# Dilated attention: mixing weights broadcast through a DRAM scratch instead of by selector products

## The chip, the cores and the metric

The kernel runs on one core of one Trainium2 chip. What counts is the time of one execution on the device, in microseconds; the median of several runs is given. The core has TensorE (matrix products), VectorE, ScalarE, GpSimd, and SyncE, whose queue issues nearly all DMA transfers.

## The reference

Two layers of a hybrid attention block over 512 tokens of width 1024. A layer normalises x, multiplies it by one wide matrix, runs three attentions, gates and merges them, and adds the result to x. The change is in the third attention, the dilated mixture: three groups of four heads (64 wide) attend with different windows and strides, and their outputs are mixed per token and head by a softmax over the three groups' log-sums:

```python
C_GROUPS = ((128, 1), (512, 4), (2048, 16))
def dilated_mixture(q, k, v):
    outs, lses = [], []
    for g, (window, dil) in enumerate(C_GROUPS):
        o, l = dilated_group(q[:, :, sl], k[:, :, sl], v[:, :, sl], window // dil, dil)
        outs.append(o); lses.append(l)
    w = jax.nn.softmax(jnp.stack(lses, axis=0), axis=0)      # 3 groups x tokens x 4 heads
    return jnp.sum(w[..., None] * jnp.stack(outs, axis=0), axis=0).astype(q.dtype)
...
    yc = dilated_mixture(...).reshape(bsz, seq, C_WIDTH) * jax.nn.silu(c_g)
    merged = (gates[:, :, 0] * (ya @ w_br_a) + gates[:, :, 1] * (yb @ w_br_b) + gates[:, :, 2] * (yc @ w_br_c))
    return x + merged @ w_out
```

## The kernel before

All large products are made of three: both operands are split into a high part (rounded to the product's format) and a low part, and hi*hi, lo*hi and hi*lo are added up in PSUM (lines 430 to 432 for blocks of 128 features by 512 tokens). Activations stand transposed, features on the partitions, tokens along the row. Weights come from DRAM as `ws` tiles (4 buffers) by SyncE's queue, ScalarE (sometimes VectorE) casts them to `whi`, and GpSimd (sometimes VectorE) subtracts to get `wlo`; `whi` and `wlo` have 7 buffers each, so weights run ahead of the products by a few tiles. Products go to PSUM buffers: three for blocks (`pp`), two for scores (`sc`), two for transposes (`tp`), one for attention outputs (`pv`).

The order of the instructions is not written by hand. The kernel lists its operations with an engine, an assumed duration, what they read and write and a priority; a planner (class `Plan`) plays them through, always taking the operation that can start first, and the engines' instruction streams are emitted in the order it found. Each engine, and SyncE's queue, works its stream strictly in order. Operations of the attentions have their own priorities, projections and merges ("fills") take the room between them, and weight loads come first on SyncE (priority about -1e5).

Within a layer the units follow this list: `CV K I V Q D0 D1 A1 CW T C01 C00 gC gA gB A0 AB0 AB1 AB2 AA0 AA1 VR C1 C2 A2 AA2 B1 B0 MX B2`. MX (`c_mix`) is the mixing. For each group g and pair of heads pr there is an output `U[g][pr]`, 128 partitions (two heads of 64) by 512 tokens. The weights are worked out with tokens on the partitions (tile C, 12 columns per 128 tokens), and four transposes give them as 12 rows by 512 tokens in PSUM (`tpm`, line 1080). To multiply U by them, each row has to stand on all 64 partitions of its head. Before the change the 12 rows are split into `rw` (high part in rows 0 to 11, low part in rows 32 to 43, the rest zeroed), and a product with a constant selector of zeros and ones puts two rows onto 64 partitions each:

```python
bc = buf("sc", [P, T], F32, "bc")
nc.tensor.matmul(bc.t, sel.t[0:64, 2 * g + pr, :], rw.t[0:64], start=True, stop=True)   # L1094
add("dve", n_dve(T), lambda u=u, bc=bc: vt(u.t, u.t, bc.t, ALU.mult), r=[u, bc], w=[u], pri=pri)
```

That is six products a layer, each followed by VectorE's multiply from PSUM (line 1064). GpSimd then adds the three U of a pair, multiplies by the gate, and the result is split into `yh` and `yl`, the operands of branch B2. Around the mixing TensorE works on the gates and products of branch B0 (gate blocks of 24 products, branch products of 9); VectorE's line 873 merges them.

The selector `sel` is set up once near the start: three tiles zeroed, six small loads into them, three casts.

Of the kernel before, what the change touches and what calls it, by code (L numbers as in the profile page):

```python
# [16 lines left out]
P = 128  # L17
T = 512
# [196 lines left out]
def n_act(n, fn=False):  # L215
    return 0.84 * n + (290 if fn else 165)


def n_pool(n):
    return 2.15 * n + 190  # L220
# [3 lines left out]
def hybrid_kernel(ctx: ExitStack, tc, x, norm_g, w_in, w_br_a, w_br_b, w_br_c, w_out, final_norm_g,  # L224
# [13 lines left out]
    def buf(tag, shape, dt=F32, name="t"):  # L238
        counter[0] += 1
        return Buf(tag, shape, dt, f"{name}_{counter[0]}")  # L240

    def fixed(shape, dt, name):
        b = Buf(None, shape, dt, name)
        b.t = sb.tile(shape, dt, name=name, tag=name)
        return b
# [8 lines left out]
    tri = fixed([P, T], F32, "tri")  # L254
    band = fixed([P, 256], F32, "band")
    res = fixed([P, P], F32, "res")
    sel = fixed([P, 6, P], FR, "sel")
    scol = fixed([P, 1], F32, "scol")
    invd = fixed([P, 4], F32, "invd")
    big = fixed([P, 1], F32, "big")  # L260
    x1 = tc.dram_tile([T, D], F32, name="x1")
    vdram = [tc.dram_tile([T, T], F32, name=f"vd{l}") for l in range(DEPTH)]
    vdtok = [[token(f"vd{l}{t}") for t in range(4)] for l in range(DEPTH)]
    x1tok = [[token(f"x1_{t}{b}") for b in range(2)] for t in range(4)]
# [40 lines left out]
            add("act", 60, lambda: nc.scalar.dma_start(ident.t, k_ident), w=[ident], pri=-7e5, lag=3200.0)  # L305
    for b, k in ((cos, k_cos), (sin, k_sin), (tri, k_tri), (band, k_band), (res, k_res)):
        dma(lambda b=b: b.t, lambda k=k: k, b, 300, pri=50)
    for g in range(3):

        s32 = buf("u", [P, 2, P], F32, "s32")  # L310
        add("pool", 300, lambda s32=s32: nc.gpsimd.memset(s32.t, 0.0), w=[s32], pri=50)
        for p0 in (4 * g, 32 + 4 * g):
            dma(lambda s32=s32, p0=p0: s32.t[p0:p0 + 4], lambda: k_sel[32:36], s32, 300, pri=50)
        add("act", n_act(256), lambda g=g, s32=s32: nc.scalar.copy(sel.t[:, 2 * g:2 * g + 2, :], s32.t), r=[s32], w=[sel], pri=50)
    add("pool", 100, lambda: nc.gpsimd.memset(scol.t[0:64], -0.125), w=[scol])
    add("pool", 100, lambda: nc.gpsimd.memset(scol.t[64:128], 1.0), w=[scol])
    add("pool", 100, lambda: nc.gpsimd.memset(invd.t, 1.0 / D), w=[invd])
# [430 lines left out]
    def layer(l):  # L748
# [306 lines left out]
        def c_mix(gC):  # L1055
# [24 lines left out]
                    nc.tensor.transpose(tp.t[0:12, i, :], C.t[:, 12 * i:12 * i + 12], ident.t)  # L1080
            add("pe", n_mm(4, P), ft, r=[C, ident], w=[tp], pri=pri, name="mixT")

            rw = buf("u", [P, T], FR, "rw")
            add("pool", n_pool(T) / 2, lambda: nc.gpsimd.memset(rw.t[0:64].bitcast(F32), 0.0), w=[rw], pri=pri, after=plan.ops[-1:])
            split(lambda: tp.t[0:12].rearrange("p b n -> p (b n)"), tp, lambda: rw.t[0:12], rw, lambda: rw.t[32:44], rw, T, pri, True)
            ys = []
            for pr in range(2):
                acc = None
                for g in range(3):
                    pri = apri()  # L1090
                    bc = buf("sc", [P, T], F32, "bc")

                    def fb(pr=pr, g=g, bc=bc):
                        nc.tensor.matmul(bc.t, sel.t[0:64, 2 * g + pr, :], rw.t[0:64], start=True, stop=True)  # L1094
                    add("pe", n_mm(1, T), fb, r=[rw, sel], w=[bc], pri=pri, name="bc")
                    u = U[g][pr]
                    add("dve", n_dve(T), lambda u=u, bc=bc: vt(u.t, u.t, bc.t, ALU.mult), r=[u, bc], w=[u], pri=pri)
                    if acc is None:
                        acc = u
                    else:  # L1100
                        tt(T, lambda acc=acc: acc.t, lambda acc=acc: acc.t, lambda u=u: u.t, ALU.add, [u, acc], [acc], pri, "cadd")
                tt(T, lambda acc=acc: acc.t, lambda acc=acc: acc.t, lambda pr=pr: gC[pr].t, ALU.mult, [acc, gC[pr]], [acc], pri, "cgate")
                yh, yl = buf("u", [P, T], FR, "yh"), buf("u", [P, T], FR, "yl")
                split(lambda acc=acc: acc.t, acc, lambda yh=yh: yh.t, yh, lambda yl=yl: yl.t, yl, T, pri)
                ys.append((yh, yl))
# [127 lines left out]
```

## Time and profile before

| | |
|---|---|
| median of 3 runs | 1074.54 us (1073.83 to 1074.83) |
| profiled execution, its own time | 1073.64 us |
| its span, first to last instruction | 1071.9 us |
| TensorE busy / weight loads | 1062.5 us / 885.9 us |
| VectorE, ScalarE, GpSimd busy | 510.9, 592.0, 637.5 us |
| granted TensorE clock | 0.998 of full |
| moved by DMA | 119.00 MB |

The span is that of the one execution that was profiled; its own time is the device time of the same execution. Busy times are sums of the instructions' durations; a product's recorded duration (about 390 ns for 512 columns) overlaps with the next one's, so the distance between two starts is what a product takes.

### The profile page before, as it was taken

To read this page: it belongs to the slowest core of one execution; us is meant where nothing else is said; L and a number is where in the kernel's file an instruction comes from. 1 tells how busy PE (TensorE), PEld (TensorE's weight loads), DVE (VectorE), ACT (ScalarE), POOL (GpSimd) and SP (SyncE) were. 2 spreads that over 40 slices of the span, in tenths; PEclk is the share of its full clock that TensorE was granted. 3 is DMA by queue.
4 is the path that set the end of the run, shared out by engine and by line. 5 is a ranking of instruction groups with operands and counts; after the bars stand their busy time and mean duration, and the time that the engine had idled before them with its cause. 6 is when DMAs were issued, how large, how long until landed. Compare 5 with 4: busy or idle time off the path is not lost.

```text
span 1071.9 us, 16877 instructions
## 1 busy us (share of the span) xinstructions
PE 1062.5 (99%) x5390; PEld 885.9 (83%) x5390; DVE 510.9 (48%) x1434; ACT 592.0 (55%) x1493; POOL 637.5 (59%) x636
## 2 busy tenths in 40 slices
PE   9999999999999999999999999999999999999997
PEld 5898888888887878888888889888888878788885
DVE  5138987566642441113432589856655425311143
ACT  6444356787776653334553444568877767333441
POOL 4765754557753349776666177545666425686853
PEclk9999999999999999999999999999999999999999
DMA  7653543433431323453754155334444223336322
GB/s 227 186 125 79 148 109 83 140 83 94 120 94 51 81 60 99 110 175 98 217 160 130 30 136 145 85 95 112 112 101 119 65 52 81 87 89 194 109 81 78
DMA packets 123690, 119.00 MB, mean 111 GB/s; under 512 B 19385, under 2 KB 102225, under 8 KB 123602
## 3 DMA queue, kind: packets, MB, share of 16 engines
q1 hardware_dynamic: 123312, 117.61, 40.3%
q8 instruction: 42, 0.69, 0.3%
q14 instruction: 46, 0.38, 0.1%
q10 hardware_dynamic: 290, 0.33, 0.1%
HBM read 96.07 MB, written 6.36 MB: 96 GB/s over the span
## 4 chain that ended last, share of the span: by engine, by line
PE 98%; ACT 1%; issue 1%; DVE 0%; POOL 0%; POOLq 0%
PE pp L430 22%; PE pp L432 21%; PE pp L431 21%; PE sc L542 4%; PE pp L451 3%; PE pp L450 3%; PE pp L449 3%; PE po L1150 3%; PE po L1149 3%; PE po L1151 3%; PE tp L614 2%; PE pv L637 2%; PE pv L649 1%; PE sc L999 1%; PE pv L1037 1%; PE tpn L717 1%
## 5 line engine op out<-in xcount | busy, mean ns | idle before, releaser
L337 POOL TENSOR_TENSOR wlo<-ws,whi 128x256 fp32r<-128x256 f32 (+2 forms) x439 | 439.4, 1016 | 314.7 <-ACT whi L331 260.9
L430 PE MATMUL pp<-h_hi,whi 128*128 128x512 f32 (+1 forms) x896 | 357.1, 399 | 0.4 <-DVE gate L526 0.3
L432 PE MATMUL pp<-h_hi,wlo 128*128 128x512 f32 (+1 forms) x896 | 348.4, 389 | 0.0
L431 PE MATMUL pp<-h_lo,whi 128*128 128x512 f32 (+1 forms) x896 | 348.2, 389 | 0.0
L331 ACT CAST whi<-ws 128x256 fp32r<-128x256 f32 (+2 forms) x434 | 214.7, 508 | 236.1 <-PE pp L431 123.8
L432 PEld LDWEIGHTS pp<-h_hi,wlo 128*128 128x128 f32 x896 | 168.2, 188 | 35.1
L430 PEld LDWEIGHTS pp<-h_hi,whi 128*128 128x128 f32 x896 | 168.5, 188 | 34.3 <-issue 3.5
L431 PEld LDWEIGHTS pp<-h_lo,whi 128*128 128x128 f32 x896 | 168.6, 188 | 28.7
L873 DVE SCALAR_TENSOR_TENSOR th<-th,pp 128x512 f32<-128x512 f32 x32 | 22.0, 687 | 132.0 <-PE pp L432 126.8
L390 DVE TENSOR_TENSOR ptl<-tp,pth 128x256 fp32r<-128x256 f32 (+3 forms) x128 | 58.1, 462 | 44.0 <-ACT pth L331 43.3
L449 PE MATMUL pp<-whi,h_hi 128*128 128x512 f32 (+2 forms) x192 | 67.5, 352 | 0.0
L451 PE MATMUL pp<-whi,h_lo 128*128 128x512 f32 (+2 forms) x192 | 66.8, 348 | 0.0
L450 PE MATMUL pp<-wlo,h_hi 128*128 128x512 f32 (+2 forms) x192 | 66.7, 347 | 0.0
L331 ACT CAST pth<-tp 128x256 fp32r<-128x256 f32 (+3 forms) x128 | 50.7, 406 | 26.1 <-PE tp L614 15.0
L858 ACT ACTIVATE th<-pp 128x512 f32<-128x512 f32 x48 | 28.6, 595 | 54.6 <-PE pp L432 54.6
L552 ACT ACTIVATE p<-p,st 128x128 f32<-128x128 f32 (+3 forms) x96 | 53.5, 558 | 1.8 <-DVE st L550 1.5
L609 ACT ACTIVATE p<-p,st 128x128 f32<-128x128 f32 (+3 forms) x96 | 50.9, 558 | 1.8 <-DVE st L608 1.4
L820 DVE MATCH_REPLACE8 work<-m,work 128x512 f32<-128x512 f32 (+2 forms) x96 | 51.8, 542 | 0.1
L819 DVE MAX8 m<-work 128x8 f32<-128x512 f32 (+2 forms) x96 | 50.8, 550 | 0.7 <-POOL work L812 0.4
L430 PE MATMUL pp<-yh,whi 128*128 128x512 f32 x128 | 50.7, 396 | 0.0
L1149 PE MATMUL po<-whi,mhh 128*128 128x512 f32 x128 | 50.2, 392 | 0.0
L432 PE MATMUL pp<-yh,wlo 128*128 128x512 f32 x128 | 50.0, 391 | 0.0
(189 smaller groups left out, 1732.3 us busy)
## 6 DMA issues: line engine op xcount, KB each, us to landing
ws<-in_w_in_dram SPq DMA_DIRECT2D x192, 256.0 KB, 2.9
ws<-in_w_in_dram SPq DMA_DIRECT2D x96, 128.0 KB, 2.3
ws<-in_w_out_dram SPq DMA_DIRECT2D x32, 256.0 KB, 2.6
ws<-in_w_in_dram SPq DMA_DIRECT2D x24, 192.0 KB, 2.9
x<-x SPq DMA_DIRECT2D x16, 256.0 KB, 3.9
x<-in_x_dram SPq DMA_DIRECT2D x15, 256.0 KB, 5.1
zq<-rt SPq DMA_DIRECT2D x48, 64.0 KB, 2.8
zq<-rt SPq DMA_DIRECT2D x20, 128.0 KB, 2.4
```

The lines of the kernel that those rows point to most:

```text
L331: add("act", n_act(n), lambda: nc.scalar.copy(dst(), src()), r=r, w=w, pri=pri, name=name, alt=("dve", n_dve(n, two), lambda: nc.vector.te ...
L337: add("pool", n_pool(n), lambda: nc.gpsimd.tensor_tensor(dst(), a(), b(), op), r=r, w=w, pri=pri, name=name, alt=("dve", n_dve(n), lambda: ...
L390: add("dve", n_dve(n), lambda: nc.vector.tensor_tensor(lo_fn(), src_fn(), hi_fn().bitcast(F32), ALU.subtract), r=[src, hi] if hi is not lo ...
L430: nc.tensor.matmul(o, lhs(hi.t, k % 2), a, start=(k == 0), stop=False)
L431: nc.tensor.matmul(o, lhs(hi.t, k % 2), b, start=False, stop=False)
L432: nc.tensor.matmul(o, lhs(lo.t, k % 2), a, start=False, stop=(k == nk - 1))
L449: nc.tensor.matmul(ps.t[:, :width], tokfn(h_hi, k), hi.t[:, kk, :width], start=(k == 0), stop=False)
L450: nc.tensor.matmul(ps.t[:, :width], tokfn(h_hi, k), lo.t[:, kk, :width], start=False, stop=False)
L451: nc.tensor.matmul(ps.t[:, :width], tokfn(h_lo, k), hi.t[:, kk, :width], start=False, stop=(k == KD - 1))
L552: add("act", n_act(N, True) + 190, lambda: nc.scalar.activation(p.t[:, :N], p.t[:, :N], AF.Exp, bias=nm_fn(), scale=-1.0, accum_out=s_fn() ...
L820: add("dve", n_dve(N) + 80, lambda i=i, N=N: nc.vector.match_replace(works[i].t[:, :N], m8[i].t, works[i].t[:, :N], GONE), r=[works[i], m8 ...
L1149: nc.tensor.matmul(ps.t[:, :n], mh.t[:, c], hi.t[:, kk, :n], start=(k == 0), stop=False)
```

## The change

The 12 mixing rows are copied to SBUF as they are, without a split. They are stored to a scratch in DRAM (`wdram`, one for each layer, 12 rows of 512), and for each group and pair two loads read a row each for the 64 partitions of its head into an SBUF tile `bc`, which VectorE multiplies into U. The selector, its set-up and the six products a layer go.

```diff
-    sel = fixed([P, 6, P], FR, "sel")
...
+    wdram = [tc.dram_tile([12, T], F32, name=f"wd{l}") for l in range(DEPTH)]
...
-    for g in range(3):
-
-        s32 = buf("u", [P, 2, P], F32, "s32")
-        add("pool", 300, lambda s32=s32: nc.gpsimd.memset(s32.t, 0.0), w=[s32], pri=50)
-        for p0 in (4 * g, 32 + 4 * g):
-            dma(lambda s32=s32, p0=p0: s32.t[p0:p0 + 4], lambda: k_sel[32:36], s32, 300, pri=50)
-        add("act", n_act(256), lambda g=g, s32=s32: nc.scalar.copy(sel.t[:, 2 * g:2 * g + 2, :], s32.t), r=[s32], w=[sel], pri=50)
...
-            rw = buf("u", [P, T], FR, "rw")
-            add("pool", n_pool(T) / 2, lambda: nc.gpsimd.memset(rw.t[0:64].bitcast(F32), 0.0), w=[rw], pri=pri, after=plan.ops[-1:])
-            split(lambda: tp.t[0:12].rearrange("p b n -> p (b n)"), tp, lambda: rw.t[0:12], rw, lambda: rw.t[32:44], rw, T, pri, True)
+            rw, rows = buf("u", [P, T], F32, "rw"), token("rows")
+            copy(T, lambda: rw.t[0:12], lambda: tp.t[0:12].rearrange("p b n -> p (b n)"), [tp], [rw], pri, "rw")
+            add("sp", 650, lambda: nc.sync.dma_start(wdram[l], rw.t[0:12]), r=[rw], w=[rows], pri=-3e4, lag=2000.0)
             ys = []
             for pr in range(2):
                 acc = None
                 for g in range(3):
                     pri = apri()
-                    bc = buf("sc", [P, T], F32, "bc")
-
-                    def fb(pr=pr, g=g, bc=bc):
-                        nc.tensor.matmul(bc.t, sel.t[0:64, 2 * g + pr, :], rw.t[0:64], start=True, stop=True)
-                    add("pe", n_mm(1, T), fb, r=[rw, sel], w=[bc], pri=pri, name="bc")
+                    bc = buf("u", [P, T], F32, "bc")
+                    for f in range(2):
+                        dma(lambda bc=bc, f=f: bc.t[64 * f:64 * f + 64],
+                            lambda n=4 * g + 2 * pr + f: wdram[l][n:n + 1, :].to_broadcast([64, T]), bc, 450, r=[rows], pri=-3e4)
                     u = U[g][pr]
                     add("dve", n_dve(T), lambda u=u, bc=bc: vt(u.t, u.t, bc.t, ALU.mult), r=[u, bc], w=[u], pri=pri)
```

## Rows read from the trace of the kernel before

**Rows 1.** The page: busy times, and the chain that ended last by engine
```profile
PE 1062.5 (99%) x5390; PEld 885.9 (83%) x5390; DVE 510.9 (48%) x1434; ACT 592.0 (55%) x1493; POOL 637.5 (59%) x636
...
PE 98%; ACT 1%; issue 1%; DVE 0%; POOL 0%; POOLq 0%
```

**Rows 2.** Timeline of TensorE (start, duration, instruction), 406 to 418 us
```profile
406.77 0.39 PE L432 MATMUL pp<-yh,wlo 128*128 128x512 f32 x1
...
417.88 0.39 PE L430 MATMUL pp<-yh,whi 128*128 128x512 f32 x1
```

**Rows 3.** Timeline of TensorE, 392.6 to 402.1 us
```profile
392.60 0.39 PE L431 MATMUL pp<-h_lo,whi 128*128 128x512 f32 x1
...
393.16 0.73 PE L1094 MATMUL bc<-rw,sel 64*128 64x512 f32 x2
393.82 0.50 PE L430 MATMUL pp<-h_hi,whi 128*128 128x512 f32 x1
...
402.01 0.39 PE L432 MATMUL pp<-h_hi,wlo 128*128 128x512 f32 x1
```

**Rows 4.** Stretches: busy PE, PEld, DVE, ACT, POOL; clock, DMA share, GB/s
```profile
392.00:401.00 9.00, 9.00 (x34) 5.56 (x33) 4.78 (x8) 2.81 (x6) 5.74 (x6) 1.00 0.05 16
...
407.00:418.00 11.00, 11.00 (x50) 9.13 (x49) 0.69 (x1) 3.31 (x7) 10.72 (x10) 1.00 0.22 65
```

**Rows 5.** Timeline of SyncE's queue, 385 to 401 us
```profile
387.88 11.74 SPq L284 DMA_DIRECT2D ws<-in_w_br_a_dram  x2
```

**Rows 6.** DMA issues: tile, queue, count, KB each, median us to landing
```profile
zc<-rt SPq DMA_DIRECT2D x32, 64.0 KB, 2.1
...
zc<-rx SPq DMA_DIRECT2D x16, 128.0 KB, 2.5
...
sd<-stc SPq DMA_DIRECT2D x4, 16.0 KB, 1.4
```

**Rows 7.** Tile bc: ns min/median/max, first and last start; waits before (us, times)
```profile
L1094 PE MATMUL bc<-rw,sel x12: 387/497/502, 393.2 to 925.1; 64*128 64x512 f32 x12
L1064 DVE TENSOR_TENSOR U<-U,bc x12: 679/687/689, 393.7 to 925.7; 128x512 f32<-128x512 f32 x12
...
who waited for it (us, times):
...
  PEld bc L1094: 1.4, 4
```

**Rows 8.** Tile rw
```profile
L331 ACT CAST rw<-tpm x2: 575/575/575, 390.0 to 915.5; 12x512 fp32r<-12x512 f32 x2
```

**Rows 9.** Timeline of TensorE, 28 to 51 us
```profile
28.57 0.39 PE L449 MATMUL pp<-whi,h_hi 128*128 128x512 f32 x1
...
50.12 0.39 PE L432 MATMUL pp<-h_hi,wlo 128*128 128x512 f32 x1
```

**Rows 10.** Tile gb (the norm's gain): issue ns, and landing of its transfers
```profile
L284 SPq DMA_DIRECT2D gb<-in_norm_g_dram x2: 463/476/488, 517.9 to 518.4; - x2
...
DMA to landing us min/median/max: 5.0/5.4/6.4
```

**Rows 11.** Line 338: ns min/median/max, first and last start
```profile
L338 DVE TENSOR_TENSOR mg<-mg,th x8: 685/1232/1811, 492.3 to 1025.2; 128x512 f32<-128x512 f32 x8
```

**Rows 12.** Timeline of VectorE, 400 to 406 us
```profile
400.17 0.69 DVE L1064 TENSOR_TENSOR U<-U,bc 128x512 f32<-128x512 f32 x1 [0.97 <-PE bc L1094]
405.15 0.69 DVE L873 SCALAR_TENSOR_TENSOR th<-th,pp 128x512 f32<-128x512 f32 x1 [4.29 <-PE pp L432]
```

**Rows 13.** Timeline of GpSimd, 402 to 427 us
```profile
402.23 2.65 POOL L337 TENSOR_TENSOR wlo<-ws,whi 128x512 fp32r<-128x512 f32 x2 [0.48 <-ACT whi L331]
...
411.75 2.68 POOL L337 TENSOR_TENSOR U<-U,U 128x512 f32<-128x512 f32 x2
414.51 5.37 POOL L337 TENSOR_TENSOR wlo<-ws,whi 128x512 fp32r<-128x512 f32 x4
...
425.53 1.30 POOL L337 TENSOR_TENSOR yl<-U,yh 128x512 fp32r<-128x512 f32 x1
```

**Rows 14.** Timeline of TensorE, 441 to 463 us, first product of B2
```profile
462.75 0.39 PE L430 MATMUL pp<-yh,whi 128*128 128x512 f32 x1
```

## Prediction

> **What bounds the kernel now.** I read the page first: the engines' busy times and the chain of work that ended last [rows 1]. TensorE is busy 99% of the span and holds 98% of the chain, so only two things change the time: work that TensorE no longer does, and work that arrives too late for it. The profiled execution took 1073.64 us with a span of 1071.9 us; the median of the three runs is 1074.54 us, 0.9 us above it. The sum below is made on the profiled execution and carried over to the median as a difference.
>
> "Busy" does not prove that TensorE streams at its best, so next I read its timeline. A 512-column product of the projections starts one step after the one before it: between the two rows of [rows 2] lie 49 steps in 11.11 us, 0.2267 us each. That is the undisturbed step. Then I read TensorE's timeline around the six broadcast products (bc) of the first layer [rows 3], and, for what the new transfers meet, the table of stretches [rows 4], SyncE's queue [rows 5] and the DMA table [rows 6].
>
> **What is removed from TensorE.** From 392.60 to 402.01 us [rows 3] TensorE starts 28 ordinary 512-column products and the six bc. The 28 cost 28 x 0.2267 = 6.35 us; the stretch took 9.41 us. So six bc cost 3.06 us, 0.51 us each, over twice a step. Part of it shows directly: from the first pair's start at 393.16 to the next ordinary product at 393.82 go 0.66 us, where two steps would be 0.45. Another part is a wait: the weight loads of bc stood 1.4 us in four places for VectorE's multiply [rows 7], which has to free one of two PSUM buffers first. The second layer shows the same pattern 525.5 us later (bc start between 393.2 and 925.1 [rows 7]), so I count twice: 6.1 us. Lower bound: only streaming comes back, 12 x 0.2267 = 2.7 us. Upper bound: the whole 6.1, as nothing else was lost in the stretch. I take the upper one, because every product of the stretch was counted and only the bc break the step.
>
> **What is removed elsewhere.** The selector's set-up (three copies on ScalarE, three memsets, six small loads), VectorE's two "lo" subtractions and GpSimd's two memsets of rw. No engine but TensorE ends the chain, and where the selector was built TensorE already ran without a gap: from 28.57 to 50.12 us are 21.55 us, 95 steps of 0.2267 [rows 9]. All this counts nothing. Without that cover the six issues, at 0.48 us each [rows 10], would be worth at most 2.9 us.
>
> **What is added.** Per layer: one store of 24 KB to the scratch, twelve loads of 128 KB (64 partitions read one 2 KB row), and a wait of the loads on the store. The copy of the transposed weights stays (575 ns on ScalarE [rows 8]). None of it is on TensorE. In the first layer the copy is done at 390.0 + 0.6 = 390.6 us. Nearest rows for the store: the statistics' store, 1.4 us from issue to landing, and a 64 KB load, 2.1 [rows 6]; so it is there at 392.1 to 392.8. Nearest rows for the loads: plain 128 KB ones land in 2.5 us [rows 6], and the norm's gain, which also reads DRAM rows for many partitions, takes 0.48 us to issue and up to 6.4 us to land for 256 KB [rows 10]. Twelve issues take 5.7 us, the last at 397.5 to 398.2 (issue time counted once), landing 2.5 to 6.4 us later: 400.0 to 404.6. I take about 401, nearer to the rows of the same size. The last multiply then takes 0.69 us as now, or 1.81 us, the longest of VectorE's sums of two SBUF tiles [rows 11]: it ends at 400.7 to 406.4, against 400.17 + 0.69 = 400.86 now [rows 12]. It is late by nothing to 5.5 us.
>
> Queues passed. SyncE issued one weight load at 387.88, and its next one only some 11.4 us later (two issues in 11.74 us [rows 5]), at about 399.2, since a staging buffer had to come free. The 13 new issues fit into that hole, 390.6 to 398.2, and the DMA engines were 5% busy from 392 to 401 [rows 4]. Behind the first broadcast, which waits on SyncE for the store, stand the other eleven and then that weight load, due at 399.2. On VectorE the multiplies now wait for a DMA, and behind them stands the merge of 405.15 [rows 12]. A merge frees one of three PSUM product buffers; this one is free at 405.84 and wanted again after the product block that ends at 407.0 and a gate block of 24 steps, at 412.4: 6.6 us of cover. On GpSimd the sums of U wait for the multiplies, and behind these stand the weight splits (wlo). The two splits that end at 404.9 [rows 13] make the last two of four weight tiles of the block that starts at 407.0; the fourth is wanted 18 steps later, at 411.1: 6.2 us of cover. The four from 414.51 [rows 13], the first done at 415.8, are wanted from 421.96 on (products start at 417.88 [rows 2], 18 steps): 6.1 us. The result itself, yl, done at 426.8 [rows 13], is first wanted at 462.75 [rows 14]: 36 us.
>
> So lateness up to about 6.1 us per layer costs nothing, and what is late next would be GpSimd's splits.
>
> **A row against it.** The multiply read one operand from PSUM and took 679 to 689 ns in all twelve cases [rows 7]; now both come from SBUF. VectorE's sum of mg and th, both in SBUF, took 685 to 1811 ns [rows 11] where GpSimd worked beside it. If GpSimd stands for the whole of each multiply, that is 6 x 0.69 = 4.1 us per layer, below the 6.1, so the sum stays. The Trainium skill, page "SBUF — State Buffer", section "Who interferes with whom", says that a VectorE instruction with two SBUF inputs contends with a GpSimd instruction that reads SBUF, and that the later one waits for the other to end. The trace's 685 to 1811 ns agrees with it. By that rule the sum would be unchanged too unless the transfers are late as well, which is rival A.
>
> **Sum.** TensorE -6.1 us, the rest +0 behind its cover: 1073.64 to 1067.5 for a profiled execution, 1074.54 to 1068.4 for the median.
>
> **Rivals.** (A) GpSimd gets late beyond its cover: it is busy 10.72 of 11 us from 407 to 418 [rows 4] and can't catch up there. Multiplies 2.7 us late (the middle of 0 and 5.5), 4.1 us of standing, and one split of 1.3 us pushed behind a sum are 8.1 us; TensorE loses 8.1 - 6.1 = 2.0 us per layer, which gives 1068.4 + 4.0 = 1072.4. Against it: the second pair's sums ran on GpSimd only at 411.75 [rows 13], 10.9 us after their last multiply, so a late second pair need not hold it. Chance 0.10.
>
> (B) Slower: the same queue at its worst. The multiplies end 5.5 us late with GpSimd's sums queued ahead of the splits, and 4.1 us of standing and one split of 1.3 us come on top: 10.9 us. TensorE loses 4.8 us per layer, 9.6 in all, against 6.1 gained: 1078.0. It decides from 6.1 + 3.06 = 9.2 us of lateness per layer on. For it: the gain's 6.4 us. Against it: that was among other traffic, and every upper bound has to come together. Chance 0.05.
>
> (C) Only streaming comes back, because something else breaks the step in that stretch, say VectorE's or ScalarE's in-order work: 1074.54 - 2.7 = 1071.8. Against it: the ordinary products between the bc keep their step. Chance 0.07.
>
> (D) Not felt: the planner orders the whole program anew, and may put the weight load of 399.2 in front of the store on SyncE. The store then goes out 8.6 us late, after 399.2, and the last multiply is as late; that is 2.5 beyond the cover, 5.0 for two layers, leaving 1.1 of the 6.1: 1073.4. Against it: the store is ready 8.6 us before that load's buffer. Chance 0.06.
>
> **How the numbers follow.** The forecast has the remaining 0.72; its own range is 1067.0 to 1070.0, as the new order may move up to 1.5 us at the start or the layer boundary. The range 1066.5 to 1072.5 takes in A and C as well; B, D and 0.05 of the forecast (a larger reshuffle) stay out, 0.16. A difference of 0.2%, 2.1 us, is about what a measurement here can tell from no change. Faster: the forecast, C and most of A, 0.87; within it D and the rest of A, 0.07; slower, B and a little of the reshuffle, 0.06.
>
> **What would show it.** In the changed profile: twelve products fewer, and ordinary products a steady 0.227 us apart where the bc were; the second layer's mixing about 3 us earlier, the end 6; the twelve loads issued in SyncE's hole and landing in 2 to 5 us; multiplies of 0.7 to 1.8 us. Wrong would be: TensorE waiting for whi, wlo or a PSUM buffer between 400 and 430 us, a store issued after 392 us, or a last multiply that ends after 407.

## The result, and the profile after

The changed kernel takes 1067.39 us (median of five runs, 1066.87 to 1068.14), where the kernel before took 1074.54 in the same comparison: a ratio of 0.9937, with an interval of 0.9925 to 0.9948. That is 7.15 us less; the forecast was 6.1 less, 1068.4. The profiled executions tell nearly the same: the span went from 1071.9 to 1065.1 us, 6.8 less.

First the page of the kernel after: busy times, and the chain that ended last by engine.

```profile
PE 1054.9 (99%) x5378; PEld 884.4 (83%) x5378; DVE 515.9 (48%) x1432; ACT 590.6 (55%) x1490; POOL 640.3 (60%) x631
...
PE 97%; ACT 1%; DVE 1%; issue 1%; DMA 0%; POOL 0%; POOLq 0%; ACTq 0%; DVEq 0%
```

TensorE has twelve products fewer (5378 against 5390 [rows 1]) and is still what sets the end. Next its timeline where the bc were: the last step before the new stretch, the end of that gate block, and the first products of the two blocks whose weight tiles were the concern.

```profile
392.48 0.40 PE L425 MATMUL pp<-h_hi,wlo 128*128 128x512 f32 x1
...
399.29 0.39 PE L425 MATMUL pp<-h_hi,wlo 128*128 128x512 f32 x1
...
403.60 0.39 PE L423 MATMUL pp<-h_hi,whi 128*128 128x512 f32 x1
...
418.56 0.39 PE L423 MATMUL pp<-h_hi,whi 128*128 128x512 f32 x1
```

From the first to the second row are 30 steps in 6.81 us, 0.227 each: nothing breaks the step any more. The block that started at 407.0 before starts at 403.60. Going through the whole timeline, the four transposes ahead of the mixing start at 389.0 (389.4 before), the first layer's first output product (po) at 492.0 (495.4 before), and the last product of all at 1057.8 (1064.2). So 0.4 us was there before the mixing began, nearly all of it by the first projection product (14.39 against 14.69); 3.0 came from the first mixing and 3.0 from the second; the last 0.4 of the span's 6.8 fell behind the last product. The two mixings make 6.0 to 6.1 us, and what lies beyond them is no part of the mechanism.

SyncE's queue after (start, time that the group took, instruction and count), where before there was one weight load at 387.88 and then a hole [rows 5]:

```profile
390.24 0.38 SPq L1078 DMA_DIRECT2D wd<-rw  x1
391.84 6.77 SPq L284 DMA_DIRECT2D bc<-wd  x10
398.71 0.54 SPq L284 DMA_DIRECT2D ws<-in_w_br_a_dram  x1
399.35 1.08 SPq L284 DMA_DIRECT2D bc<-wd  x2
```

The store goes out at 390.24 and the first broadcast 1.6 us later. Ten loads fit the hole; the planner put the next weight load, at 398.71, ahead of the last two.

Tile bc after: issues, multiplies, idle time before them, and landing.

```profile
L284 SPq DMA_DIRECT2D bc<-wd x24: 444/587/1137, 391.8 to 923.1; - x24
L1057 DVE TENSOR_TENSOR U<-U,bc x12: 677/1278/1779, 395.2 to 926.5; 128x512 f32<-128x512 f32 x12
...
  DMA bc<-wd: 8.2, 7
...
DMA to landing us min/median/max: 2.8/2.9/3.8
```

VectorE's timeline after, the six multiplies of the first layer and the merges (th) behind them:

```profile
395.23 0.69 DVE L1057 TENSOR_TENSOR U<-U,bc 128x512 f32<-128x512 f32 x1 [2.07 <-DMA bc<-wd]
396.63 1.68 DVE L1057 TENSOR_TENSOR U<-U,bc 128x512 f32<-128x512 f32 x1 [0.71 <-DMA bc<-wd]
398.75 6.36 DVE L1057 TENSOR_TENSOR U<-U,bc 128x512 f32<-128x512 f32 x4 [0.44 <-DMA bc<-wd]
405.03 1.27 DVE L866 SCALAR_TENSOR_TENSOR th<-th,pp 128x512 f32<-128x512 f32 x2
```

The last multiply ends at 405.1, 4.2 us later than the 400.86 of before. The wait was exchanged for a slower multiply: 0.677 to 1.779 us, where all twelve took 679 to 689 ns before [rows 7]. GpSimd's timeline after, with the splits (wlo) that TensorE waits for next:

```profile
399.43 1.74 POOL L330 TENSOR_TENSOR U<-U,U 128x512 f32<-128x512 f32 x1
401.12 3.44 POOL L330 TENSOR_TENSOR wlo<-ws,whi 128x512 fp32r<-128x512 f32 x2
...
414.41 5.05 POOL L330 TENSOR_TENSOR wlo<-ws,whi 128x512 fp32r<-128x512 f32 x4
```

The two splits end at 402.8 (half of 3.44 after 401.12) and 404.56, a little earlier than before (403.5 and 404.9 [rows 13]). Only the first of the two belongs to the block that starts at 403.60. The kernel loads four full weight tiles (128x512) for a pair of gate blocks, and then one full tile and one half (128x256) for the branch products; the second split is that full branch tile. In a gate block a tile serves six products, and the third of the six is the first to read its low part. So the fourth tile's split is wanted 20 steps after 403.60, at 408.1, 5.3 us after it is done. (The run with three detours below shows both: TensorE stops at just this product, and goes on when the first of the two splits is done.) Before, it was done at 403.5 and wanted 20 steps after 407.0, at 411.5: 8.0 us. In the second block the first of the four splits is the second tile's, by the order of the loads. It is done at about 415.7 (a quarter of 5.05 after 414.41) and wanted 8 steps after 418.56, at 420.4: 4.7 us are left, of 8.0 before (415.8, and 8 steps after 421.96).

The shortest cover lies elsewhere. The first merge starts right behind the last multiply and is done at 405.7 (half of 1.27 after 405.03). It frees the product buffer in PSUM that TensorE wants for the second gate block, 24 steps after 403.60, at 409.0. That leaves 3.3 us, where the prediction had counted 6.6.

The table of stretches after shows who works beside whom (busy PE, PEld, DVE, ACT, POOL; granted clock, DMA share, GB/s):

```profile
392.00:400.00 8.00, 8.00 (x37) 6.60 (x36) 4.46 (x6) 3.50 (x7) 5.50 (x5) 1.00 0.47 163
405.00:414.00 9.00, 9.00 (x41) 7.47 (x40) 1.31 (x3) 2.61 (x5) 9.00 (x8) 1.00 0.32 91
```

The transfers are no small matter (the DMA engines were 5% busy here before [rows 4], now 47%), and GpSimd has no pause from 405 to 414. Neither reaches TensorE.

### The profile page after: what moved, and what is told of

It reads as the page before. It is cut to its first block, busy times and chain, and to the rows that moved or that the text cites. A ratio compares the mean times of both kernels' runs of the same rounds, so it can differ in the third digit from the quotient of the medians.

```text
span 1065.1 us, 16874 instructions
## 1 busy us (share of the span) xinstructions
PE 1054.9 (99%) x5378; PEld 884.4 (83%) x5378; DVE 515.9 (48%) x1432; ACT 590.6 (55%) x1490; POOL 640.3 (60%) x631
## 2 busy tenths in 40 slices
DMA packets 125611, 122.18 MB, mean 115 GB/s; under 512 B 19769, under 2 KB 102585, under 8 KB 125522
## 4 chain that ended last, share of the span: by engine, by line
PE 97%; ACT 1%; DVE 1%; issue 1%; DMA 0%; POOL 0%; POOLq 0%; ACTq 0%; DVEq 0%
PE pp L423 22%; PE pp L425 22%; PE pp L424 22%; PE sc L535 4%; PE pp L444 3%; PE pp L443 3%; PE pp L442 3%; PE po L1143 3%; PE po L1142 3%; PE po L1141 3%; PE tp L607 2%; PE pv L630 2%; PE pv L642 1%; PE sc L992 1%; PE pv L1030 1%; PE tpn L710 1%
```

## The experiments

Each ratio is to the kernel before, run on the same chip in the same comparison; "changes after" means that the experiment's kernel is the changed one with one edit.

| run | what it is | this, us | before, us | ratio (interval) |
|---|---|---|---|---|
| e1_setup_kept | changes after: selector built, unread | 1067.84 | 1073.78 | 0.9941 (0.9926 to 0.9956) |
| e2_layer0_only | scratch in the first layer alone | 1071.05 | 1073.78 | 0.9970 (0.9960 to 0.9980) |
| e3_rows128 | changes before: bc over 128 rows | 1070.62 | 1073.78 | 0.9972 (0.9961 to 0.9982) |
| e4_twice | changes before: each bc twice | 1076.68 | 1073.78 | 1.003 (1.002 to 1.004) |
| e5_psum_operand | changes after: bc copied to PSUM | 1067.35 | 1074.59 | 0.9934 (0.9919 to 0.9949) |
| e6_late_once | changes after: one detour by DRAM | 1068.29 | 1074.59 | 0.9942 (0.9925 to 0.9958) |
| e7_late_three | changes after: three detours | 1081.33 | 1074.59 | 1.0062 (1.0047 to 1.0077) |
| e8_six_loads | changes after: one load per bc | 1109.35 | 1074.59 | 1.0332 (1.0315 to 1.035) |
| e10_six_loads_16 | the same, rows kept 8 times | 1067.67 | 1074.12 | 0.9939 (0.9925 to 0.9954) |
| e11_six_loads_4 | the same, rows kept twice | 1080.18 | 1074.12 | 1.0055 (1.0038 to 1.0073) |
| e9_no_transposes | changes after: weights stored untransposed | 1118.37 | 1074.12 | 1.040 (1.0375 to 1.0426) |
| e12_scores_rows128 | changes after: scores over 128 rows | 1071.62 | 1073.95 | 0.9976 (0.9967 to 0.9986) |

### Does the set-up count, and is it once per layer?

In the first run the three memsets, six loads and three copies of the selector are put back into the changed kernel, where nothing reads their result.

```diff
+    sel = fixed([P, 6, P], FR, "sel")
...
+    for g in range(3):
+        s32 = buf("u", [P, 2, P], F32, "s32")
+        add("pool", 300, lambda s32=s32: nc.gpsimd.memset(s32.t, 0.0), w=[s32], pri=50)
+        for p0 in (4 * g, 32 + 4 * g):
+            dma(lambda s32=s32, p0=p0: s32.t[p0:p0 + 4], lambda: k_sel[32:36], s32, 300, pri=50)
+        add("act", n_act(256), lambda g=g, s32=s32: nc.scalar.copy(sel.t[:, 2 * g:2 * g + 2, :], s32.t), r=[s32], w=[sel], pri=50)
```

> The changed kernel with the selector's set-up put back (three memsets, six small loads, three copies); nothing reads it. Theory 1 (the whole gain is the bc products' 0.51 us each on TensorE): the set-up was under TensorE's unbroken stream, so the time stays at that of the changed kernel, 1067.4 us within 1 us, about 6 to 7 us under the kernel before. Theory 2 (only the 2.7 us of streaming came from the products, the rest from the set-up that is gone and a better start): the time goes back up by 3 to 4 us, to about 1071.

The gain stays whole, 1067.84 against 1067.39, and the intervals of the two ratios overlap. The set-up is worth nothing that stands out of that noise, well under the 3 to 4 us of the other theory, which falls.

In the second run the scratch is used in the first layer as in the changed kernel, and the second layer keeps memset, split and products as before.

```diff
-            rw, rows = buf("u", [P, T], F32, "rw"), token("rows")
+            if l == 0:
+                rw, rows = buf("u", [P, T], F32, "rw"), token("rows")
...
+            else:
+                rw = buf("u", [P, T], FR, "rw")
...
+                    if l == 0:
+                        bc = buf("u", [P, T], F32, "bc")
...
+                    else:
+                        bc = buf("sc", [P, T], F32, "bc")
```

> The scratch in the first layer only; the second keeps the split, the selector and its six products. Theory 1: half the gain, 3.06 us, all in the first layer's mixing stretch: about 1071.2 us, and the second layer's six bc again take 3.06 us together. Theory 2: only 1.4 us of streaming is gained and the set-up is back: about 1073.

It gains 2.7 us, where the first run, on the same chip, gained 5.9 with both layers: about half. TensorE's timeline of this run in the second layer has the broken step back.

```profile
915.90 0.73 PE L1106 MATMUL bc<-rw,sel 64*128 64x512 f32 x2
916.56 0.50 PE L431 MATMUL pp<-h_hi,whi 128*128 128x512 f32 x1
```

The gain is made per layer, at the products.

### Why did a bc cost 0.51 us, twice a step?

A bc contracts over 64 rows, the ordinary products over 128. The prediction put a part of its price down to a wait of 1.4 us for VectorE's multiply [rows 7]. In the third run the kernel before has its bc run over all 128 rows (the added rows are zero in both operands), and nothing else is changed.

```diff
-            add("pool", n_pool(T) / 2, lambda: nc.gpsimd.memset(rw.t[0:64].bitcast(F32), 0.0), w=[rw], pri=pri, after=plan.ops[-1:])
+            add("pool", n_pool(T) / 2, lambda: nc.gpsimd.memset(rw.t.bitcast(F32), 0.0), w=[rw], pri=pri, after=plan.ops[-1:])
-                        nc.tensor.matmul(bc.t, sel.t[0:64, 2 * g + pr, :], rw.t[0:64], start=True, stop=True)
+                        nc.tensor.matmul(bc.t, sel.t[:, 2 * g + pr, :], rw.t, start=True, stop=True)
```

> The kernel before, with the selector products over all 128 rows (rows 44 to 127 of rw zeroed, the selector is zero there already) in place of 64; waits unchanged. If the part of a bc beyond its step (0.40 us at each of four visits a layer) comes from the change between 64-row and 128-row weights, it shrinks: up to 4 x 0.3 us a layer, so 1 to 2.4 us faster than the kernel before. If it comes from the wait on the multiply and the copy, which is the same here, the time stays within 0.5 us of the kernel before.

It gains 3.2 us with all twelve products still there. TensorE's timeline of this run, from the last ordinary product but one ahead of the first pair, with a single bc, to the first product after the 28 ordinary ones:

```profile
392.40 0.39 PE L431 MATMUL pp<-h_lo,whi 128*128 128x512 f32 x1
...
392.86 0.63 PE L1094 MATMUL bc<-rw,sel 128*128 128x512 f32 x2
393.33 0.40 PE L430 MATMUL pp<-h_hi,whi 128*128 128x512 f32 x1
...
394.72 0.40 PE L1094 MATMUL bc<-rw,sel 128*128 128x512 f32 x1
394.95 0.40 PE L430 MATMUL pp<-h_hi,whi 128*128 128x512 f32 x1
...
400.26 0.39 PE L432 MATMUL pp<-h_hi,wlo 128*128 128x512 f32 x1
```

A pair takes 0.47 us and a single one 0.23: a step each. The stretch with the same 28 ordinary products and six bc takes 7.86 us; less 28 x 0.2267 = 6.35 that is 1.51 for six, where it was 3.06 [rows 3]. The multiply behind each bc is the same, and so are its two PSUM buffers. So half of what a bc cost was its 64-row form, between neighbours of 128 rows. The weight loads (PEld) of bc show where it went, two of them in the kernel before and then a pair in this run:

```profile
393.16 0.29 PEld L1094 LDWEIGHTS bc<-rw,sel 64*128 64x128 f32 x2 [0.36 <-issue]
395.40 0.18 PEld L1094 LDWEIGHTS bc<-rw,sel 64*128 64x128 f32 x1 [0.36 <-DVE U L1064]
```

```profile
392.63 0.42 PEld L1094 LDWEIGHTS bc<-rw,sel 128*128 128x128 f32 x2
```

With 64 rows the load stands for 0.36 us and starts together with its product (393.16 both); with 128 rows it starts 0.23 us ahead of its product at 392.86 and stands for nothing. And it stands for the same 0.36 us whether the profile names VectorE's multiply or nothing ("issue"): the 1.4 us in four places of [rows 7] have a twin of 1.4 us in four places with no wait at all. The multiply had no part in it that can be seen.

The fourth run keeps the 64-row form and issues each product twice.

```diff
-                        nc.tensor.matmul(bc.t, sel.t[0:64, 2 * g + pr, :], rw.t[0:64], start=True, stop=True)
-                    add("pe", n_mm(1, T), fb, r=[rw, sel], w=[bc], pri=pri, name="bc")
+                        for _ in range(2):
+                            nc.tensor.matmul(bc.t, sel.t[0:64, 2 * g + pr, :], rw.t[0:64], start=True, stop=True)
+                    add("pe", n_mm(2, T), fb, r=[rw, sel], w=[bc], pri=pri, name="bc")
```

> The kernel before with every bc product issued twice in a row into the same buffer. Theory 1 as worked out from the rows (a step of 0.2267 for each product and about 0.40 us for each visit): 12 x 0.2267 = 2.7 us slower than the kernel before, 1077.3. If each product costs 0.51 us by itself, 6.1 us slower, 1080.7.

It loses 2.9 us, not 6. Some 2.0 of them are in the two mixings; 1.0 lies at the layer boundary, where TensorE waits 1.03 us for the norm at 529.37, as it does not in the kernel before, and where that comes from was not looked into. Its timeline, around one of the visits that TensorE pays to the 64-row form:

```profile
392.65 0.40 PE L432 MATMUL pp<-h_hi,wlo 128*128 128x512 f32 x1
392.98 1.21 PE L1095 MATMUL bc<-rw,sel 64*128 64x512 f32 x4
394.11 0.50 PE L430 MATMUL pp<-h_hi,whi 128*128 128x512 f32 x1
394.45 0.40 PE L431 MATMUL pp<-h_lo,whi 128*128 128x512 f32 x1
```

The four products of a visit take 1.13 us to the next ordinary product, 0.22 more than four steps. Another 0.21 lies in the 0.33 us from the ordinary product before to the first bc and the 0.34 from the first ordinary product after to the second. No weight load of a bc waits for a multiply in this run, and each visit pays all the same. The planner made three visits a layer here, where the kernel before makes four. The price per visit, from the stretches of the first layer: here 12 products and 28 ordinary ones take 10.41 us (392.42 to 402.83), and (10.41 - 40 x 0.2267) / 3 = 0.45; in the kernel before (9.41 - 34 x 0.2267) / 4 = 0.43 [rows 3]. One price, 0.43 to 0.45 us a visit, and a step for each product explain this stretch in both kernels. A price of 0.51 per product does not: it would have made this run 6 us slower.

### Does VectorE's multiply stand behind GpSimd?

In the fifth run ScalarE copies each bc into PSUM, so that the multiply reads one operand from SBUF as it did before; ScalarE's twelve copies of 0.59 us come on top.

```diff
+                    bs, bc = bc, buf("sc", [P, T], F32, "bp")
+                    add("act", n_act(T), lambda bs=bs, bc=bc: nc.scalar.copy(bc.t, bs.t), r=[bs], w=[bc], pri=pri, name="bp")
```

> The changed kernel with ScalarE copying each bc tile to PSUM (the two score buffers) before VectorE's multiply, so that the multiply has one operand in SBUF again. Theory 1 (the slow multiplies and GpSimd's longer instructions are real but lie behind the cover): multiplies back at 0.68 to 0.69 us, GpSimd's sums of U at 1.3 us in place of 1.74, and the time as the changed kernel's, 1067.4 us within 1 us. Rival (the two-operand form costs time on the path): 1 to 4 us faster than the changed kernel.

Tile bp of this run, and GpSimd's sum that took 1.74 us in the changed kernel:

```profile
L1057 DVE TENSOR_TENSOR U<-U,bp x12: 680/689/690, 397.3 to 928.5; 128x512 f32<-128x512 f32 x12
```

```profile
399.44 1.30 POOL L330 TENSOR_TENSOR U<-U,U 128x512 f32<-128x512 f32 x1
```

All twelve multiplies are back at 0.69 us, and GpSimd's sum is 0.44 faster. So the two engines do hold each other up when the multiply has two SBUF operands, and the time does not show it: 1067.35 against 1067.39. The Trainium skill, page "SBUF — State Buffer", section "Who interferes with whom", says so of a VectorE instruction with two SBUF inputs beside a GpSimd instruction that reads SBUF; the trace agrees with it, 0.69 against 1.28 us (medians).

### How late may the weights be?

Two runs send the rows on detours: stored to DRAM and loaded back once, or three times (range(3)), before the store to the scratch.

```diff
+            for k in range(1):
+                gone, back = token("gone"), buf("u", [P, T], F32, "rw")
+                add("sp", 10, lambda k=k, rw=rw: nc.sync.dma_start(wlate[l][k], rw.t[0:12]), r=[rw], w=[gone], pri=-3e4)
+                add("sp", 10, lambda k=k, back=back: nc.sync.dma_start(back.t[0:12], wlate[l][k]), r=[gone], w=[back], pri=-3e4)
+                rw = back
```

> The changed kernel with the 12 rows taken once more to DRAM and back before the scratch is stored; the planner is told next to nothing of the time, so the order stays close. The rows come some 4 us later. Theory 1 with the cover read from the changed profile (splits done 2.9 to 3.2 us ahead of their products): time up by 0 to 3 us, 1067.4 to 1070.5. Rival (the mixing's result has 36 us of cover, and nothing behind it in a queue matters): no change.

The first broadcast is issued at 395.72, 3.9 us later than in the changed kernel, and the time is 1068.29, a ratio within the interval of the changed kernel's. Four microseconds of lateness are nearly covered. In the first layer TensorE does not stop for it; in the second it stops once where the changed kernel does not:

```profile
942.75 0.50 PE L424 MATMUL pp<-h_hi,whi 128*128 128x512 f32 x1 [0.84 <-ACT th L852]
```

The product waits for a PSUM buffer that ScalarE's tanh (th) frees, and on ScalarE the tanh stands behind weight casts and the cast of U (yh, at 940.02), which had waited 5.79 us for GpSimd. That costs about 1 us, by a way that the prediction did not name.

> As the run before with three round trips in place of one: the rows come some 12 us later. Theory 1: GpSimd's queue stands for the sums of U, the splits behind it are late and TensorE waits about 12 - 3 = 9 us a layer at the most: 1073 to 1086 us, with TensorE idle on wlo between 400 and 430 us. Rival (36 us of cover): still 1067.4.

The first broadcast is issued at 402.26, 10.4 us later, and the time is 1081.33, 14 us above the changed kernel and slower than the kernel before. Its rows show the way that the prediction had named for it. GpSimd, then TensorE, in the first layer:

```profile
408.06 1.29 POOL L331 TENSOR_TENSOR U<-U,U 128x512 f32<-128x512 f32 x1 [8.39 <-DVE U L1058]
409.30 3.40 POOL L331 TENSOR_TENSOR wlo<-ws,whi 128x512 fp32r<-128x512 f32 x2
```

```profile
404.51 0.39 PE L424 MATMUL pp<-h_hi,whi 128*128 128x512 f32 x1
...
411.07 0.52 PE L426 MATMUL pp<-h_hi,wlo 128*128 128x512 f32 x1 [1.86 <-POOL wlo L331]
...
413.90 0.79 PE L424 MATMUL pp<-h_hi,whi 128*128 128x512 f32 x1 [1.03 <-DVE th L867]
```

GpSimd's sum waits 8.39 us for the multiply, the split queued behind the sum is late, and TensorE stops for it; then TensorE stops for VectorE's merge (th), which is queued behind the multiplies. The product at 411.07 is the one 20 steps after the block's start at 404.51, due at 409.0, and it starts when the first of the two splits is done (half of 3.40 after 409.30). The waits on wlo sum to 4.8 us over the execution and those on th to 1.8, less than half of the 14. The rest is in the main the clock, in the table of stretches (columns as above):

```profile
414.00:420.00 6.00, 6.00 (x18) 4.75 (x19) 1.47 (x2) 0.34 (x1) 6.00 (x6) 0.65 0.48 142
```

After it had stood still TensorE was granted 0.65 of its clock in this stretch. From 412 to 417 us alone it was 0.50, the lower of its two levels (1.2 of 2.4 GHz), and its products come 0.43 us apart until 417.90; from 418.30 on they come 0.23 apart. 18 products stand in the stretch, where 26 steps of 0.2267 fit; the missing eight and a half steps are 1.9 us. Product by product against the changed kernel, the first layer's two blocks lose 6.1 us, 3.5 of them at the two stops and 2.6 in slow steps, and the second layer's lose 6.7. That is 12.8 of the 14; 0.9 is there at the start of the stream.

### Could half of the twelve loads do?

A bc tile needs two rows, each for 64 partitions. The eighth run loads both with one transfer, whose source begins with a dimension of two rows.

```diff
-                    for f in range(2):
-                        dma(lambda bc=bc, f=f: bc.t[64 * f:64 * f + 64],
-                            lambda n=4 * g + 2 * pr + f: wdram[l][n:n + 1, :].to_broadcast([64, T]), bc, 450, r=[rows], pri=-3e4)
+                    dma(lambda bc=bc: bc.t, lambda n=4 * g + 2 * pr: wdram[l][n:n + 2, :].rearrange("f (o t) -> f o t", o=1).to_broadcast([2, 64, T]), bc, 450, r=[rows], pri=-3e4)
```

> The changed kernel with one load of two rows onto 128 partitions for each bc in place of two loads onto 64. Theory 1: SyncE needs half the issues, the last multiply ends some 2 us earlier, GpSimd's lateness falls, and the time stays at the changed kernel's 1067.4 us within 1 us since nothing of it was on TensorE's path. Rival (SyncE's issues delay the weight loads): 1 to 3 us faster.

No theory had this: 1109.35 us, 42 above the changed kernel. The stretch from 400 to 405 us of this run, and the wait of TensorE that followed:

```profile
400.00:405.00 5.00, 5.00 (x24) 4.14 (x23) 0.68 (x1) 1.12 (x2) 0.00 (x0) 1.00 0.13 49
```

```profile
428.53 0.79 PE L423 MATMUL pp<-h_hi,whi 128*128 128x512 f32 x1 [17.29 <-DVE th L866]
```

The DMA engines are 13% busy, which is two of sixteen, at 49 GB/s, while VectorE does nothing but wait for bc (its multiplies start 5.35 us apart: 256 KB at 49 GB/s). TensorE stood 17 us for the merge behind the multiplies, in each layer. To see whether it is the outermost dimension that decides, the rows were kept in the scratch several times, so that the same single load begins with 16 or with 4:

```diff
-    wdram = [tc.dram_tile([12, T], F32, name=f"wd{l}") for l in range(DEPTH)]
+    wdram = [tc.dram_tile([12, 8, T], F32, name=f"wd{l}") for l in range(DEPTH)]
-            add("sp", 650, lambda: nc.sync.dma_start(wdram[l], rw.t[0:12]), r=[rw], w=[rows], pri=-3e4, lag=2000.0)
+            for c in range(8):
+                add("sp", 400, lambda c=c: nc.sync.dma_start(wdram[l][:, c, :], rw.t[0:12]), r=[rw], w=[rows], pri=-3e4, lag=2000.0)
...
+                    dma(lambda bc=bc: bc.t, lambda n=4 * g + 2 * pr: wdram[l][n:n + 2].rearrange("f c (o t) -> (f c) o t", o=1).to_broadcast([16, 8, T]), bc, 450, r=[rows], pri=-3e4)
```

(8 copies give 16; 2 copies, broadcast as `[4, 32, T]`, give 4.)

> Six loads onto 128 partitions again, but the scratch holds each row 8 times (8 stores), so that a load's outermost count is 16 and not 2. If the outermost count of 2 held each of the slow loads to 2 of the 16 DMA engines, they now spread: a load lands in about 3 to 4 us, the time is back near the changed kernel's, 1067.4 us, or up to 2 us more for the eight stores. If it was the size or the 128 partitions of the load, it stays near 1109.

> The same with each row held twice: outermost count 4. If the count is the number of DMA engines at work, a load takes half the 5.35 us that lay between two landings with a count of 2, about 2.7 us, six of them 16 us a layer in place of 32: the time lies between, 1072 to 1085 us. If the count doesn't matter, 1109.

The stretch from 400 to 403 us, first of the run with 16, then of the run with 4:

```profile
400.00:403.00 3.00, 3.00 (x15) 2.49 (x14) 2.29 (x4) 1.12 (x2) 2.37 (x2) 1.00 1.03 256
```

```profile
400.00:403.00 3.00, 3.00 (x15) 2.47 (x14) 0.69 (x1) 1.12 (x2) 1.22 (x1) 1.00 0.26 96
```

Outermost 2, 4 and 16 give a DMA share of 0.13, 0.26 and 1.03, at 49, 96 and 256 GB/s, and 1109, 1080 and 1067.7 us. The Trainium skill, page "DMA: Bandwidth & Descriptors", section "Rules for kernel authors", has this rule: an outermost dimension below 16 confines a transfer to at most that many DMA engines. These rows agree with it. With 16, six loads and eight stores are as good as twelve loads and one store, and no better.

### Could the transposes go too?

The ninth run leaves out the four transposes and the copy, and stores the weights, tokens on the partitions, straight into the rows of the scratch.

```diff
-            tp = buf("tp", [P, 4, P], F32, "tpm")
...
-            rw, rows = buf("u", [P, T], F32, "rw"), token("rows")
...
-            add("sp", 650, lambda: nc.sync.dma_start(wdram[l], rw.t[0:12]), r=[rw], w=[rows], pri=-3e4, lag=2000.0)
+            rows = token("rows")
+            for i in range(4):
+                add("sp", 650, lambda i=i: nc.sync.dma_start(wdram[l][:, i * P:(i + 1) * P].rearrange("j p -> p j"), C.t[:, 12 * i:12 * i + 12]), r=[C], w=[rows], pri=-3e4, lag=5000.0)
```

> The changed kernel without the four transposes a layer that turn the weights: the tile with tokens on the partitions is stored straight to the scratch by four transfers of 4-byte pieces, and the rows are read as before. It is ready some 23 us earlier than the transposes, which wait their turn in the two transpose buffers. Theory 1 (only TensorE's own work counts): the transposes took 0.36 us from the first one's start to the next product's, so 0.7 us in two layers, about 1066.7 us, hardly to be told from the changed kernel. Rival: transfers of 4-byte pieces are so slow that the rows come later than now, and the splits' 3 us of cover is lost: 1069 to 1080.

It is 4% slower than the kernel before. The stretch after the first stores, their row in the DMA table, and TensorE's largest wait:

```profile
375.00:385.00 10.00, 10.00 (x49) 8.30 (x48) 4.43 (x16) 5.61 (x16) 3.17 (x3) 1.00 1.03 1
```

```profile
wd<-mc SPq DMA_DIRECT2D x8, 6.0 KB, 21.9
```

```profile
PE tp L607 <- ACT p L602: 35.0, 4, 15.3
```

All the DMA engines are busy for 10 us at 1 GB/s. The page counts 137980 packets here and 125611 in the changed kernel, 12369 more; the weights are 12 x 512 x 2 = 12288 numbers. Each four-byte number went by itself, 6 KB took 21.9 us to land, the multiplies waited (one for 18.5 us), and the attention queued behind them on VectorE brought TensorE to a stop. The four transposes are worth the 0.36 us a layer that they take (389.00 to the next product at 389.36 in the changed kernel).

### Does the price of the 64-row form hold elsewhere?

The scores of the dilated groups 2 and 3 (line 992) are 64-row products too, one per head, which alternate between the lower and the upper 64 rows. The last run makes them 128-row products, which leaves the heads unseparated: each score is the sum of the two heads', so the output is not the reference's.

```diff
-                            nc.tensor.matmul(sc[f].t[:, b * P:(b + 1) * P], q[pr].t[r, b * P:(b + 1) * P], k[pr].t[r, b * P:(b + 1) * P],
+                            nc.tensor.matmul(sc[f].t[:, b * P:(b + 1) * P], q[pr].t[:, b * P:(b + 1) * P], k[pr].t[:, b * P:(b + 1) * P],
```

> The changed kernel with the scores of the second and third dilated group taken over all 128 rows of q and k (both heads of a pair added up, so the mixture's output changes) in place of 64: same products, same columns, same waits. If the 64-row form costs TensorE an extra at each visit, as at the bc products, the eight visits of 16 products (1.29 us each beyond the ordinary steps, of which 16 x 0.057 = 0.91 is streaming) lose most of 8 x 0.39 us: up to 3.1 us faster than the changed kernel, about 1064.5. If the extra belonged to the bc products' waits alone, no change: 1067.4.

It went the other way: 1071.62 us, 4.2 slower than the changed kernel. TensorE's timeline around one visit, first in the changed kernel, then in this run:

```profile
328.75 0.40 PE L425 MATMUL pp<-h_hi,wlo 128*128 128x512 f32 x1
329.08 1.16 PE L992 MATMUL sc<-zc,zc 64*128 64x128 f32 x16
330.17 0.50 PE L423 MATMUL pp<-h_hi,whi 128*128 128x512 f32 x1
```

```profile
331.06 0.39 PE L425 MATMUL pp<-h_hi,wlo 128*128 128x512 f32 x1
331.29 1.95 PE L992 MATMUL sc<-zc,zc 128*128 128x128 f32 x16
332.99 0.47 PE L423 MATMUL pp<-h_hi,whi 128*128 128x512 f32 x1
```

The price of the entry is gone (0.23 us to the first score, where it was 0.33), but the sixteen take 1.70 us to the next ordinary product, where they took 1.09: 0.11 each against 0.07. So the 64-row products that alternate between the two halves came faster than the 128-row ones, and that is worth more than the entry. The visit is 0.51 us longer; eight visits make 4.1 us, about the difference of the medians. (The profiled execution is 5.2 us longer in its span; 1.2 us of it are there before the first such visit, at 313.17 against 311.97. Where they come from was not looked into.)

## Why the prediction was right, and where it was not

**TensorE, -6.1 us.** Right, and by its own working: 9.41 us less 28 steps, twice [rows 3]. The two mixings gave 3.0 and 3.0. The bound that it chose, the whole of the stretch's excess over the step, was the right one; only streaming, rival C, would have been 2.7.

**The reason given for "over twice a step" was not.** The prediction took the wait of bc's weight load on the multiply [rows 7] for a part of the excess. The same loads stand as long where the profile names no wait, and with the multiply unchanged and the rows made 128 (e3), the excess of 1.70 us a layer (3.06 less six steps) shrank to 0.15. It was the 64-row form, at 0.43 to 0.45 us a visit. The sum came out right since it counted the stretch and not the causes; a prediction of the smaller change of e3 from the same reason would have been wrong.

**The set-up, 0.** Right (e1).

**The store and the loads.** The store was there after 1.6 us (1.4 to 2.1 forecast). The loads landed in 2.8 to 3.8 us, inside the 2.5 to 6.4 and near the end that was taken. The queue's order was not as forecast: the last two loads stood behind the weight load of 398.71, and were issued at 399.35 and later where 398.2 had been the latest.

**The lateness.** Forecast between nothing and 5.5 us, with a landing at 401 taken; the last multiply ended 4.2 us late. The prediction had named the first of the two causes, slower multiplies (1.28 us in the median); the other is the two late loads.

**The cover, 6.1 us.** Here the prediction was wrong in two readings, without effect on the time. First, it compared the other engines with the times at which TensorE of the kernel before wanted their work. But TensorE itself comes 3 us earlier for the lack of the bc, and every cover shrinks by that. Second, it took the second of the two splits for the block's fourth tile, and the first of the four for the next block's first tile, and it counted to a tile's first product, which does not yet read the low part. Read by the tiles, the splits had 8.0 us of cover in both blocks, not 6.2 and 6.1, and 5.3 and 4.7 were left. So the two slips work against each other: some 5 us of lateness in these splits would be free, and at 8 us the waits alone would take the whole gain. No run made only these splits late; this is worked out from the rows. The same slips are in rivals A and B, whose 6.1 us should be about 5; B's breakeven of 9.2 us should be about 8.

Nor would GpSimd's splits be alone in what is late next. The merge had the shortest cover, 3.3 us. In e11 TensorE stops for the merge in both layers, 9.4 us in all, and not once for a split; in e7 and e8 it stops for both, and in e6 for ScalarE's tanh. The detours agree: 3.9 us more for the first load cost about 1 us, 10.4 us more cost 14 and made the kernel slower than before.

The forecast held all the same since the lateness did not reach the splits, and the merge's 3.3 us sufficed. GpSimd's stream has the first pair's sum at 399.43, ahead of the two splits, and its next sum only behind them, at 404.52, so that the last multiplies make later sums wait and not these splits. That is the planner's order, for which the prediction had only the order of the kernel before; to that extent it was luck.

**The row against it.** The multiplies did stand beside GpSimd, up to 1.78 us, as the sums of mg and th did [rows 11], and e5 shows that this is worth nothing here, as the sum had it.

The 1.0 us by which the median is better than forecast (1067.39 against 1068.4) goes with the 0.4 us that the stream was earlier before the mixing began and the 0.4 behind the last product. Whether these come from the planner's new order or from the spread of the runs was not settled.

## What to carry to other kernels

Where one engine sets the time and runs at a steady step, price a removed instruction by the stretch it breaks (its length less the steps of the rest), and not by its own duration; then ask what the excess comes from before pricing a smaller edit by it. When work leaves the bounding engine, that engine also comes earlier for everything else, so the cover of every other engine shrinks by the gain: compare their finish times with the new demand, not the old one, and make sure which product reads which tile. A broadcast by way of DRAM was nearly free here behind such an engine, with an outermost dimension of 16 or more and rows of 2 KB, as long as what was queued behind the waiting instruction was not wanted soon.

## What the runs showed of the hardware that was not expected

- A 64-row product between 128-row ones cost 0.43 to 0.45 us a visit beyond its step, however many products the visit had (the kernel before, e4); its weight load stood 0.36 us and started with its product, where a 128-row one started 0.23 us ahead (e3). 64-row products that alternate between the two halves took 0.07 us each (the changed kernel) where 128-row ones took 0.11 (e12).
- The outermost dimension of a broadcast's source set how many DMA engines worked: shares of 0.13, 0.26 and 1.03 for 2, 4 and 16 (e8, e11, e10).
- Storing single four-byte numbers to DRAM filled all DMA engines at 1 GB/s (e9).
- After stops of 1.86 and 1.03 us TensorE's granted clock was 0.65 from 414 to 420 us, and its steps were 0.43 us until 417.90 (e7); the clock was 0.50 from 421 to 427 us, within a stop of 17.29 us (e8).
